# Mixing of a two-layer hybrid block: Gelus put off past the scans, steps reordered, the recurrence's elementwise steps moved from GpSimd

## The chip, the cores and the metric

One Trainium2 chip, one of its cores. The time is the device time of one execution of the program, in microseconds (us); lower is better. A core has TensorE (PE in the profile; PEld is its weight load), VectorE (DVE), ScalarE (ACT), GpSimd (POOL) and SyncE (SP, which here issues almost all transfers). Each runs its own queue of instructions in order and waits on semaphores for the others.

## What is computed

Two layers over 512 latent tokens and 256 context tokens of width 1024, all in fp32. Each layer has a token-mixing and a SwiGLU part; the change touches the mixing alone. One input projection feeds three head groups:

```python
# A: bidirectional gated recurrence on 512 channels, gated by gelu of 512 more
xc = conv4(p[..., :512])
r, i = sigmoid(xc @ wa + ba), sigmoid(xc @ wx + bx)          # per direction
a = exp(-8 * r * softplus(-lam))
h = scan(a, sqrt(1 - a*a) * (i * xc))                        # both directions, added
y_a = gelu(p[..., 512:1024]) * h
# B: chunked gating on 256 channels
u, v = gelu(p[..., 1024:1280]), gelu(p[..., 1280:1536])
y_b = u * (ws @ layer_norm(v) + bs)
# C: Fourier mixing on 256 channels
y_c = real(fft2(p[..., 1536:])) @ wf
out = concat(rms(y_a), rms(y_b), rms(y_c)) @ w_out
```

The last layer gives no context output, so its gate, u, v and Fourier parts cover the 512 latent tokens only; its recurrence covers all 768.

## The kernel before

Tokens lie in six tiles of 128. A product in fp32 is made of three products of rounded halves (`mm`, lines 195 to 200), so every operand is split into a high half (a rounding copy, mostly ScalarE's, line 208) and a low half (a subtraction, line 203). Weights are split as they come to be used; during the mixing `self.wsub` puts the low half of a weight on GpSimd, until the step `D` puts it on VectorE. PSUM holds three large tiles (`mm`, 1024 wide) and two small ones (`aux`, 512 wide).

The order of the mixing is written out by hand: `mixing` (line 959) walks the string `STEPS[l]` (line 49) and calls one step for each letter. Loads follow the same string (`plan`) and are issued by SP ahead of use, as far as the arena has room; a digit sets the room that loads must leave. The letters:

- `e`: the four gate products of one group of 128 recurrence channels, their sigmoids, and i times xc (line 751); `a`, `k`: projection, convolution and split of the fourth group; `f`: Fourier maps.
- `Z`, `V`, `U`: weights for z, v, u are taken and split. `z`: a Fourier projection, split out of PSUM (lines 819 and 820). `c`: Fourier products over channels for two tiles, split out of PSUM the same way. `v`, `u`: a projection for two tiles and its Gelu (line 921); v is then normalised on VectorE (`gating_norm`).
- `p`: Tanh and Exp of one recurrence group, both directions (`lru_scans`, lines 764 and 767). It leaves two pieces of work; `s` runs one of them: Sqrt (773), four elementwise operations (774 to 777), two scans (781 to 785); the second adds both directions (791).
- `g`: the projection of a gate, its Gelu (1000), times h (1002), squared (1003), the squares summed (1005).
- `m`: 512 columns of the modulation, 2 MB of weights, copied out of PSUM (515); the part before is then transposed and reduced (`mod_put`). `R`: two such parts become rows, added to broadcast rows of b_mod (547, loaded at line 551).
- `w`, `t`: the gating's matrices and its products (953); then come the products over positions of the Fourier part (`fourier`) and the output projection.

ScalarE holds one set of function tables at a time; Sigmoid, Tanh with Exp, Sqrt, and Gelu each need a load (ACT_TABLE_LOAD in the profile). `in_turn` and `behind` keep ScalarE's functions in the order of the steps, so that these loads stay few.

## Time and profile before

| | |
|---|---|
| median of 3 runs | 1561.46 us (1560.18 to 1562.3) |
| the profiled execution | 1561.9 us, its span 1559.8 us |
| TensorE, matmul | 1447.0 us busy (93%) |
| VectorE | 781.7 us (50%) |
| ScalarE | 531.5 us (34%) |
| GpSimd | 349.2 us (22%) |
| mean granted clock of TensorE | 0.967 |
| DMA | 163.59 MB, 105 GB/s on the mean |

The span runs from the first instruction to the last. Busy times are sums over one execution. The rows that count are further down, ahead of the prediction.

### The profile page before, as it was taken

To read this page: it belongs to the slowest core of one execution; us is meant where nothing else is said; L and a number is where in the kernel's file an instruction comes from. 1 tells how busy PE (TensorE), PEld (TensorE's weight loads), DVE (VectorE), ACT (ScalarE), POOL (GpSimd) and SP (SyncE) were. 2 spreads that over 40 slices of the span, in tenths; PEclk is the share of its full clock that TensorE was granted. 3 is DMA by queue.
4 is the path that set the end of the run, shared out by engine and by line. 5 is a ranking of instruction groups with operands and counts; after the bars stand their busy time and mean duration, and the time that the engine had idled before them with its cause. 6 is when DMAs were issued, how large, how long until landed. Compare 5 with 4: busy or idle time off the path is not lost. (4 is left out here: it accounts for less than half of the span.)

```text
span 1559.8 us, 19102 instructions
## 1 busy us (share of the span) xinstructions
PE 1447.0 (93%) x7735; PEld 1199.8 (77%) x7735; DVE 781.7 (50%) x1183; ACT 531.5 (34%) x776; POOL 349.2 (22%) x226
## 2 busy tenths in 40 slices
PE   6993998999999999999999988948898999999997
PEld 3682977788888888888888878737777788888885
DVE  6739737874323322332324386297775442543327
ACT  4574325345202202212203146854526321322210
POOL 3335512230021030020030045543321021120101
PEclk9996999999999999999999999969899999999999
DMA  9404264216106225153127004014327341432201
GB/s 321 130 1 139 85 213 173 74 65 221 55 14 212 72 96 174 55 182 111 32 79 220 14 1 135 7 41 135 103 68 238 107 135 55 128 100 78 73 0 54
DMA packets 169432, 163.59 MB, mean 105 GB/s; under 512 B 10456, under 2 KB 126648, under 8 KB 169344
## 3 DMA queue, kind: packets, MB, share of 16 engines
q1 hardware_dynamic: 169232, 162.08, 33.0%
q8 instruction: 61, 1.00, 0.3%
q0 software_dynamic: 112, 0.30, 0.1%
q14 instruction: 27, 0.22, 0.1%
HBM read 160.25 MB, written 2.10 MB: 104 GB/s over the span
## 5 line engine op out<-in xcount | busy, mean ns | idle before, releaser
L134 PE MATMUL mm<-r,r 128*128 128x512 f32 (+1 forms) x6192 | 1234.9, 360 | 18.9 <-DVE f L1138 9.2
L134 PEld LDWEIGHTS mm<-r,r 128*128 128x128 f32 x6192 | 1035.4, 191 | 214.3 <-DVE f L1138 15.0
L208 ACT ACTIVATE r<-f 128x1024 fp32r<-128x1024 f32 (+3 forms) x257 | 226.8, 908 | 626.6 <-PE mm L134 287.5
L203 DVE TENSOR_TENSOR r<-f,r 128x1024 fp32r<-128x1024 f32 (+3 forms) x262 | 275.3, 1077 | 221.0 <-ACT r L208 200.8
L203 POOL TENSOR_TENSOR f<-f,f 128x1024 f32<-128x1024 f32 (+2 forms) x68 | 153.2, 2254 | 758.1 <-DVE f L1138 565.6
L1153 DVE TENSOR_TENSOR f<-mm,f 128x768 f32<-128x768 f32 (+1 forms) x44 | 36.3, 825 | 252.8 <-PE mm L134 219.7
L1138 DVE TENSOR_TENSOR f<-mm,f 128x512 f32<-128x512 f32 (+1 forms) x80 | 76.3, 953 | 146.0 <-PE mm L134 145.9
L134 PE MATMUL aux<-r,r 128*128 128x256 f32 (+1 forms) x780 | 111.6, 304 | 39.9 <-DVE r L820 33.8
L134 PEld LDWEIGHTS aux<-r,r 128*128 128x128 f32 x780 | 105.0, 208 | 49.5 <-DVE r L820 35.7
L232 POOL TENSOR_TENSOR smalls<-smalls,neghalf 128x1 f32<-128x1 f32 (+2 forms) x69 | 65.1, 946 | 258.1 <-DVE smalls L231 255.6
L203 POOL TENSOR_TENSOR r<-f,r 128x512 fp32r<-128x512 f32 (+2 forms) x55 | 97.9, 1785 | 93.9 <-ACT r L414 28.1
L1152 ACT ACTIVATE f<-mm 128x768 f32<-128x768 f32 (+1 forms) x44 | 30.8, 700 | 121.8 <-PE mm L134 121.7
L134 PE MATMUL aux<-f,stc 128*32 128x512 f32 x384 | 51.9, 630 | 14.5 <-DVE r L820 11.3
L601 ACT ACTIVATE f<-aux,modT 128x128 f32<-128x128 f32 x128 | 48.5, 466 | 39.3 <-PE aux L134 34.8
L134 PE MATMUL aux<-cst,f 128*128 128x128 f32 (+1 forms) x243 | 37.2, 284 | 24.5 <-ACT f L586 7.8
L134 PEld LDWEIGHTS aux<-cst,f 128*128 128x128 f32 (+1 forms) x243 | 28.3, 143 | 35.3 <-ACT f L586 10.1
L586 ACT ACTIVATE f<-f,smalls 128x1024 f32<-128x1024 f32 x19 | 23.6, 1241 | 88.3 <-DVE smalls L585 88.3
L774 DVE SCALAR_TENSOR_TENSOR f<-f,f 128x768 f32<-128x768 f32 x16 | 24.7, 1543 | 45.2 <-ACT f L773 45.2
L134 PEld LDWEIGHTS aux<-f,stc 128*32 128x32 f32 x384 | 10.4, 112 | 36.8 <-issue 18.7
L719 DVE SCALAR_TENSOR_TENSOR f<-mm,par,f 128x255 f32<-128x255 f32 (+3 forms) x48 | 26.0, 607 | 15.2 <-ACT f L713 15.2
L775 POOL TENSOR_SCALAR f<-f 128x768 f32<-128x768 f32 x16 | 22.8, 1426 | 42.8 <-DVE f L774 37.7
L203 DVE TENSOR_TENSOR f<-f,f 128x512 f32<-128x512 f32 (+1 forms) x42 | 31.3, 745 | 1.5 <-ACT f L1003 0.9
(105 smaller groups left out, 641.3 us busy)
## 6 DMA issues: line engine op xcount, KB each, us to landing
f<-in_w_mod_dram SPq DMA_DIRECT2D x96, 512.0 KB
f<-in_w_up_dram SPq DMA_DIRECT2D x88, 512.0 KB
f<-in_w_down_dram SPq DMA_DIRECT2D x40, 512.0 KB
f<-in_w_in_dram SPq DMA_DIRECT2D x28, 512.0 KB
f<-in_w_out_dram SPq DMA_DIRECT2D x16, 512.0 KB
f<-in_b_mod_dram SPq DMA_DIRECT2D x6, 512.0 KB
f<-in_x_dram SPq DMA_DIRECT2D x4, 512.0 KB
f<-in_k_sinl_dram SPq DMA_DIRECT2D x4, 512.0 KB
```

The lines of the kernel that those rows point to most:

```text
L134: i = f(*args, **kw)
L203: return eng.tensor_tensor(out=out, in0=a, in1=b, op=op)
L208: i = self.nc.scalar.activation(h, src, AF.Copy)
L232: self.nc.gpsimd.tensor_tensor(out=out, in0=v, in1=self.neghalf[:, 0:n], op=ALU.pow)
L586: nc.scalar.activation(n.f, x, AF.Identity, bias=nm, scale=r)
L601: nc.scalar.activation(y.f[:, q * P : (q + 1) * P], ps[:, q * P : (q + 1) * P], AF.Identity, bias=self.modT[:, slot, k, s : s + 1], scale= ...
L719: nc.vector.scalar_tensor_tensor(out=o, in0=ps[:, i0 : i0 + o1 - o0], scalar=w(k), in1=o, op0=ALU.mult, op1=ALU.add)
L774: nc.vector.scalar_tensor_tensor(out=t_.f, in0=r.f, scalar=1.0, in1=t_.f, op0=ALU.add, op1=ALU.mult)
L775: nc.gpsimd.tensor_scalar(out=t_.f, in0=t_.f, scalar1=-1.0, scalar2=1.0, op0=ALU.mult, op1=ALU.add)
L1138: self.nc.vector.tensor_tensor(out=tb.f, in0=ps[:, c], in1=m[:, c], op=ALU.mult)
L1152: nc.scalar.activation(g.f, pg[:, 256 + lo : 1024], AF.Silu)
L1153: nc.vector.tensor_tensor(out=g.f, in0=pu[:, 256 + lo : 1024], in1=g.f, op=ALU.mult)
```

## The change

Three things. Gelus: until the new step `L` the results of gate, v and u are copied out of PSUM as they are (the new `gelu`, with `self.hold` set), and the Gelu, and what follows it, is kept in `self.late`; `L` clears the flag and does the work kept. Steps: both strings are reordered. In layer 0 two gates, the v and the u stand among the scans, the c behind `L`. In layer 1 `L` stands ahead of the first v, so nothing is kept there; its first two `s` come ahead of the second `p`. Engines: lines 751 and 791 go from GpSimd to VectorE, line 775 (1 - x) to ScalarE as an Identity with scale -1 and bias 1.

```diff
--- before.py
+++ after.py
@@ -46,7 +46,7 @@
 BETWEEN = 2
 START_RESERVE = 11000
 MIX_RESERVE = (12000, 9000)
-STEPS = ("feaekZeeppsz6szsspmpcsssmc7cgVsvvUvuuuw7DgRmgmtgmm", "faeekeeZppsszszsppVccssvsvUugDsugwgtg")
+STEPS = ("feaekZeeppzssz6ssgpgpsssVvvsvUuuumgmcLccw7DRmtgmmm", "faeekeeZpsspszzsppLcVcssvsvgUuDsugwgtg")
 PARAMS_AT = 5
 NEXT_AT = {6: 0, 7: 2, 9: 1, 10: 3, 12: 6, 13: 7, 15: 8, 16: 9, 18: 4, 19: 5}
 
@@ -748,7 +748,7 @@
         xl.free()
         for d in range(2):
             i = gates[2 * d + 1]
-            self.tt(nc.gpsimd, i.f, i.f, xc.f, ALU.mult)
+            self.tt(nc.vector, i.f, i.f, xc.f, ALU.mult)
         xc.free()
         return gates, insts
 
@@ -772,7 +772,7 @@
             s = self.buf(TOK)
             self.in_turn([nc.scalar.activation(s.f, t_.f, AF.Sqrt)])
             nc.vector.scalar_tensor_tensor(out=t_.f, in0=r.f, scalar=1.0, in1=t_.f, op0=ALU.add, op1=ALU.mult)
-            nc.gpsimd.tensor_scalar(out=t_.f, in0=t_.f, scalar1=-1.0, scalar2=1.0, op0=ALU.mult, op1=ALU.add)
+            nc.scalar.activation(t_.f, t_.f, AF.Identity, bias=self.ones[:, 0:1], scale=-1.0)
             nc.vector.scalar_tensor_tensor(out=s.f, in0=r.f, scalar=1.0, in1=s.f, op0=ALU.add, op1=ALU.mult)
             nc.vector.tensor_tensor(out=s.f, in0=s.f, in1=i.f, op=ALU.mult)
             a, u, h = t_.f, s.f, i.f
@@ -788,7 +788,7 @@
             if d == 1:
                 lo = 256 if l == DEPTH - 1 else 0
                 out = hs[m] = self.buf(TOK)
-                self.tt(nc.gpsimd, out.f[:, lo:], gates[1].f[:, lo:], h[:, lo:], ALU.add)
+                self.tt(nc.vector, out.f[:, lo:], gates[1].f[:, lo:], h[:, lo:], ALU.add)
                 gates[1].free(LRU_LAG)
                 gates[3].free(LRU_LAG)
 
@@ -910,7 +910,22 @@
             self.drop(u)
         return put
 
-    def gating_in(self, tiles, half, pair, w):
+    def gelu(self, out, ps, then=None):
+
+        nc = self.nc
+
+        def rest(src):
+            self.behind([nc.scalar.activation(out, src, AF.Gelu)], self.turn)
+            if then is not None:
+                then()
+
+        if self.hold:
+            nc.scalar.activation(out, ps, AF.Copy)
+            self.late.append(lambda: rest(out))
+        else:
+            rest(ps)
+
+    def gating_in(self, tiles, half, pair, w, then=None):
 
         z = self.buf(512)
         ps = self.psum_aux()
@@ -918,7 +933,7 @@
             for k in range(KC):
                 o = ps[:, n * 256 : (n + 1) * 256]
                 self.mm(o, self.lhs_tok(tiles[2 * pair + n], k), tuple(x[:, k % 4, :] for x in w[k // 4]), k == 0, k == KC - 1)
-        self.behind([self.nc.scalar.activation(z.f, ps, AF.Gelu)], self.turn)
+        self.gelu(z.f, ps, (lambda: then(z)) if then is not None else None)
         return z
 
     def gating_norm(self, pair, z, vb):
@@ -980,7 +995,7 @@
                 parts[blk] = self.mod_part(l, blk)
 
         self.gw, gt, work, bd = [], [], [], []
-        self.turn = []
+        self.turn, self.late, self.hold = [], [], True
         done = {"e": 0, "p": 0}
 
         zt, zc, uv, ws = [], [], {"v": [], "u": []}, []
@@ -997,13 +1012,16 @@
             self.drop(u)
             g = self.buf(TOK)
             sq.append(g)
-            self.behind([nc.scalar.activation(g.f[:, lo:], ps[:, 256 + lo : 1024], AF.Gelu)], self.turn)
-            y = hs[m]
-            nc.vector.tensor_tensor(out=y.f[:, lo:], in0=y.f[:, lo:], in1=g.f[:, lo:], op=ALU.mult)
-            nc.scalar.activation(g.f[:, lo:], y.f[:, lo:], AF.Square)
-            if m > 0:
-                self.tt(nc.gpsimd if m < MA - 1 else nc.vector, sq[0].f[:, lo:], sq[0].f[:, lo:], g.f[:, lo:], ALU.add)
-                g.free()
+
+            def rest():
+                y = hs[m]
+                nc.vector.tensor_tensor(out=y.f[:, lo:], in0=y.f[:, lo:], in1=g.f[:, lo:], op=ALU.mult)
+                nc.scalar.activation(g.f[:, lo:], y.f[:, lo:], AF.Square)
+                if m > 0:
+                    self.tt(nc.gpsimd if m < MA - 1 else nc.vector, sq[0].f[:, lo:], sq[0].f[:, lo:], g.f[:, lo:], ALU.add)
+                    g.free()
+
+            self.gelu(g.f[:, lo:], ps[:, 256 + lo : 1024], rest)
 
         def step(x):
             if x in "ZVU":
@@ -1053,6 +1071,10 @@
                     self.mod_rows(parts.pop(4 + hf), hf, m2, not last)
             elif x == "t":
                 self.gating(tiles, uv["u"], vb, ws)
+            elif x == "L":
+                self.hold = False
+                while self.late:
+                    self.late.pop(0)()
             elif x == "D":
                 self.wsub = nc.vector
             elif x == "g":
@@ -1064,9 +1086,7 @@
                     vb.extend([self.buf(n_t * 256), self.buf(n_t * 256)])
                 w = [tuple(b.r.rearrange("p (k n) -> p k n", n=256) for b in (u.high, u.low)) for u in held[x]]
                 pair = len(uv[x])
-                uv[x].append(self.gating_in(tiles, x, pair, w))
-                if x == "v":
-                    self.gating_norm(pair, uv["v"][pair], vb)
+                uv[x].append(self.gating_in(tiles, x, pair, w, (lambda z: self.gating_norm(pair, z, vb)) if x == "v" else None))
                 if pair == n_t // 2 - 1:
                     for u in held[x]:
                         self.drop(u)
```

How the instructions stand now, in three places. In these rows a name such as `f_768_746` is an arena buffer (columns, then a number given at its creation); `r_` names hold halves for products; `aux` and `mm` are PSUM. Line numbers of the changed kernel are some 1 to 20 higher behind the new function: 923 is the plain copy, 918 the Gelu, 1018 the old 1002.

ScalarE, layer 0, from the first group's Sqrts on, before:

```order
L773 ACTIVATE f_768_632<-f_768_880 128x768
L773 ACTIVATE f_768_1012<-f_768_884 128x768
L773 ACTIVATE f_768_1020<-f_768_886 128x768
L764 ACT_TABLE_LOAD
L764 ACTIVATE f_768_1030<-f_768_811,spl 128x768
L767 ACTIVATE f_768_811<-f_768_811,spl 128x768
L819 ACTIVATE r_768_640<-mm 128x768
L764 ACTIVATE f_768_1032<-f_768_829,spl 128x768
L767 ACTIVATE f_768_829<-f_768_829,spl 128x768
L764 ACTIVATE f_768_1063<-f_768_866,spl 128x768
L515 ACTIVATE f_512_1059<-aux 128x512
L764 ACTIVATE f_768_1061<-f_768_848,spl 128x768
```

And with the change:

```order
L773 ACTIVATE f_768_1020<-f_768_886 128x768
L775 ACTIVATE f_768_880<-f_768_880,ones 128x768
L208 ACTIVATE r_1024_1030<-f_1024_459 128x1024
L819 ACTIVATE r_768_640<-mm 128x768
L208 ACTIVATE r_1024_1034<-f_1024_190 128x1024
L764 ACT_TABLE_LOAD
L764 ACTIVATE f_768_746<-f_768_829,spl 128x768
L775 ACTIVATE f_768_884<-f_768_884,ones 128x768
L208 ACTIVATE r_1024_451<-f_1024_462 128x1024
L767 ACTIVATE f_768_829<-f_768_829,spl 128x768
L775 ACTIVATE f_768_886<-f_768_886,ones 128x768
L923 ACTIVATE f_768_1098<-mm 128x768
```

Weight splits (208) for the gates and for v have moved up among the Sqrts, Tanhs and Exps, each Sqrt is followed after a few rows by an Identity (775) that needs VectorE's line 774, and the plain copy of gate 0 (923) stands behind them.

VectorE, layer 0, in the second group's scans, before:

```order
L782 SCALAR_TENSOR_TENSOR f_768_770<-f_768_884,f_768_770,f_768_1012 128x512
L784 SCALAR_TENSOR_TENSOR f_768_788<-f_768_886,f_768_1020 128x256
L820 TENSOR_TENSOR r_512_1075<-aux,r_512_1074 128x512
L785 SCALAR_TENSOR_TENSOR f_768_788<-f_768_886,f_768_788,f_768_1020 128x512
L820 TENSOR_TENSOR r_512_1086<-aux,r_512_1085 128x512
L774 SCALAR_TENSOR_TENSOR f_768_1030<-f_768_811,f_768_1030 128x768
L776 SCALAR_TENSOR_TENSOR f_768_880<-f_768_811,f_768_880 128x768
L774 SCALAR_TENSOR_TENSOR f_768_1032<-f_768_829,f_768_1032 128x768
L777 TENSOR_TENSOR f_768_880<-f_768_880,f_768_820 128x768
L776 SCALAR_TENSOR_TENSOR f_768_632<-f_768_829,f_768_632 128x768
```

And with the change, the same group and the begin of the next:

```order
L781 SCALAR_TENSOR_TENSOR f_768_770<-f_768_884,f_768_1012 128x256
L777 TENSOR_TENSOR f_768_1020<-f_768_1020,f_768_788 128x768
L782 SCALAR_TENSOR_TENSOR f_768_770<-f_768_884,f_768_770,f_768_1012 128x512
L784 SCALAR_TENSOR_TENSOR f_768_788<-f_768_886,f_768_1020 128x256
L785 SCALAR_TENSOR_TENSOR f_768_788<-f_768_886,f_768_788,f_768_1020 128x512
L203 TENSOR_TENSOR f_768_1028<-f_768_770,f_768_788 128x768
L774 SCALAR_TENSOR_TENSOR f_768_1100<-f_768_811,f_768_1100 128x768
L776 SCALAR_TENSOR_TENSOR f_768_1163<-f_768_811,f_768_1163 128x768
L774 SCALAR_TENSOR_TENSOR f_768_746<-f_768_829,f_768_746 128x768
L777 TENSOR_TENSOR f_768_1163<-f_768_1163,f_768_820 128x768
```

The two splits of Fourier columns (820, out of `aux`) are gone from among the scans; the addition of both directions (203, called at 791) has come in.

ScalarE, layer 1, from the first group's Tanh on, before:

```order
L764 ACTIVATE f_768_7243<-f_768_7371,spl 128x768
L767 ACT_TABLE_LOAD
L767 ACTIVATE f_768_7353<-f_768_7353,spl 128x768
L767 ACTIVATE f_768_7371<-f_768_7371,spl 128x768
L764 ACTIVATE f_768_7513<-f_768_7391,spl 128x768
L764 ACTIVATE f_768_7515<-f_768_1061,spl 128x768
L767 ACTIVATE f_768_7391<-f_768_7391,spl 128x768
L767 ACTIVATE f_768_1061<-f_768_1061,spl 128x768
L773 ACT_TABLE_LOAD
L773 ACTIVATE f_768_7255<-f_768_7508 128x768
L773 ACTIVATE f_768_666<-f_768_7243 128x768
L819 ACTIVATE r_768_7560<-mm 128x512
```

And with the change:

```order
L767 ACT_TABLE_LOAD
L767 ACTIVATE f_768_7414<-f_768_7414,spl 128x768
L764 ACTIVATE f_768_7375<-f_768_7396,spl 128x768
L767 ACTIVATE f_768_7396<-f_768_7396,spl 128x768
L773 ACT_TABLE_LOAD
L773 ACTIVATE f_768_7557<-f_768_7375 128x768
L773 ACTIVATE f_768_7565<-f_768_7553 128x768
L764 ACT_TABLE_LOAD
L764 ACTIVATE f_768_7575<-f_768_7434,spl 128x768
L775 ACTIVATE f_768_7375<-f_768_7375,ones 128x768
L775 ACTIVATE f_768_7553<-f_768_7553,ones 128x768
L764 ACTIVATE f_768_7577<-f_768_7452,spl 128x768
```

The first two Sqrts come ahead of the second group's Tanh and Exp, with a table load more on the way back, and two Identities stand between.

## Rows read from the trace of the kernel before

**Rows 1.** The page, busy time: us, share of the span, instructions.

```profile
PE 1447.0 (93%) x7735; PEld 1199.8 (77%) x7735; DVE 781.7 (50%) x1183; ACT 531.5 (34%) x776; POOL 349.2 (22%) x226
```

**Rows 2.** Stretches: us, busy PE, PEld, DVE, ACT, POOL (instructions), clock, DMA, GB/s.

```profile
200.00:250.50 50.50, 44.68 (x273) 32.28 (x271) 25.25 (x53) 20.50 (x35) 6.92 (x8) 0.98 0.66 229
116.70:250.50 133.80, 103.20 (x676) 82.92 (x676) 95.01 (x186) 51.99 (x85) 48.99 (x28) 0.89 0.46 156
1013.05:1107.58 94.53, 61.18 (x344) 53.10 (x345) 79.23 (x137) 50.26 (x74) 40.74 (x25) 0.81 0.25 84
```

**Rows 3.** Waits of PE, 116.7 to 250.6, then 1013 to 1107.7: sum, times, longest.

```profile
PE aux L134 <- DVE r L820: 21.5, 2, 11.3
PE aux L134 <- ACT f L515: 2.6, 3, 1.4
PE aux L134 <- DMA f<-in_w_mod_dram: 2.0, 1, 2.0
PE aux L134 <- DVE r L816: 1.8, 1, 1.8
...
PE aux L134 <- DVE r L820: 23.7, 5, 10.9
```

**Rows 4.** Timeline, PE, layer 0: start, us, engine, line, operation, count, [idle before].

```profile
94.84 21.86 PE L134 MATMUL mm<-r,r 128*128 128x256 f32 x124
...
151.44 3.42 PE L134 MATMUL aux<-r,r 128*128 128x256 f32 x12 [10.15 <-DVE r L820]
```

**Rows 5.** Timeline, VectorE, layer 0's scans.

```profile
112.48 0.96 DVE L774 SCALAR_TENSOR_TENSOR f<-f,f 128x768 f32<-128x768 f32 x1 [17.56 <-ACT f L773]
...
125.85 2.55 DVE L774 SCALAR_TENSOR_TENSOR f<-f,f 128x768 f32<-128x768 f32 x1
...
129.19 1.57 DVE L776 SCALAR_TENSOR_TENSOR f<-f,f 128x768 f32<-128x768 f32 x1
...
171.05 0.93 DVE L1002 TENSOR_TENSOR f<-f,f 128x768 f32<-128x768 f32 x1
```

**Rows 6.** Groups by line, GpSimd, 95 to 172: count, busy us, mean ns, idle before.

```profile
L203 POOL TENSOR_TENSOR r<-f,r 128x1024 fp32r<-128x1024 f32 x5 | 15.2, 3052 | 3.8 <-ACT r L208 3.8
L775 POOL TENSOR_SCALAR f<-f 128x768 f32<-128x768 f32 x8 | 11.9, 1490 | 20.8 <-DVE f L774 20.8
```

**Rows 7.** Timeline, PE, layer 0: c, u, a gate, m.

```profile
140.30 0.98 PE L134 MATMUL aux<-r,r 128*128 128x256 f32 x6 [0.51 <-ACT f L515]
...
194.00 6.02 PE L134 MATMUL aux<-r,r 128*128 128x256 f32 x48 [0.34 <-ACT f L921]
...
200.22 8.60 PE L134 MATMUL mm<-r,r 128*128 128x256 f32 x48
...
237.50 1.92 PE L134 MATMUL aux<-f,stc 128*32 128x512 f32 x16
```

**Rows 8.** Timeline, ScalarE, layer 0: the first Sqrt and its table load.

```profile
110.24 1.28 ACT L773 ACT_TABLE_LOAD   x1
111.54 0.85 ACT L773 ACTIVATE f<-f 128x768 f32<-128x768 f32 x1
```

**Rows 9.** Timeline, SP and PE, layer 0: loads of b_mod's rows and step R.

```profile
198.65 1.74 SPq L551 DMA_DIRECT2D f<-in_b_mod_dram  x2
...
208.65 1.08 PE L134 MATMUL aux<-r,sel 128*128 128x512 f32 x4
```

**Rows 10.** Timeline, VectorE and PE, layer 1: the first scan step, c, a gate.

```profile
1013.33 0.96 DVE L774 SCALAR_TENSOR_TENSOR f<-f,f 128x768 f32<-128x768 f32 x1 [24.08 <-ACT f L773]
...
1022.88 1.01 PE L134 MATMUL aux<-r,r 128*128 128x256 f32 x3 [7.81 <-DVE r L820]
...
1027.47 1.86 PE L134 MATMUL aux<-r,r 128*128 128x256 f32 x7 [3.58 <-DVE r L820]
...
1040.27 2.93 PE L134 MATMUL aux<-r,r 128*128 128x256 f32 x12 [10.93 <-DVE r L820]
...
1061.08 5.63 PE L134 MATMUL mm<-r,r 128*128 128x512 f32 x24
```

## The prediction

> **What bounds the kernel now.** I read four views: the page's head, the table of stretches, the waits, the timeline. The head [rows 1] says that TensorE (PE) is the bound, busy 1447.0 of 1559.8 us; what an order can win is the rest, and what a low clock adds. The table of stretches [rows 2] finds much of it in the mixing of both layers. Layer 0, from the end of the second Fourier projection (step z) to the first product over positions: 133.8 us, PE busy 103.2 of it, at a clock of 0.89. Layer 1, likewise: 94.5 us, busy 61.2, at 0.81.
>
> The list of waits [rows 3] names what PE waits for: nearly always line 820, VectorE's low half of a split out of PSUM, 21.5 us in two waits in layer 0 and 23.7 us in five in layer 1. The timeline places them. PE's last z product ends at 94.84 + 21.86 = 116.7; after a few products it idles 11.3 us [rows 3], and before 151.44 another 10.15 [rows 4]. Its next work, the Fourier columns (step c), frees its two PSUM buffers only through line 820. That instruction stands in VectorE's queue among the scans, which run from 112.48 to 171.05 [rows 5]: 58.6 us for four channel groups, 14.6 each.
>
> Part of this is GpSimd's doing. A VectorE operation on 128x768 takes 0.95 us by itself and 2.55 beside GpSimd's addition (line 791), 1.57 beside its line 775 [rows 5]: 1.6 and 0.62 us lost each time. Per layer GpSimd does eight of 775 there, and four of 791 [rows 6]; the halves of weights that it also makes, 3.05 us each, stay with it.
>
> **The change, part by part.**
>
> *The change of the orders, layer 0.* All PE work stays; its places change. At the times at full clock [rows 7] it is 6 m of 1.92, 6 c of 0.98, 4 gates of 8.6, 6 u and v of 6.02, and about 12 us of small transposes and sums: 99.9. So the stretch now loses 133.8 - 99.9 = 33.9 us. After the change two gates and all v and u, 53 us of work that needs no VectorE result, follow the z, and the c come when the scans are through. What then is lost:
> - Gate 0's weights are split by ScalarE behind four Sqrts and two of the new Identities: from 111.54 [rows 8] six times 0.85 makes 116.6, their Copy 1 us, GpSimd 3.05: 120.7. PE waits 4.0.
> - The second v unit is split into space that the scan of group 1 gives back, and ScalarE waits for it. VectorE needs 14.6 - 2 x 0.62 - 1.6 + 0.95 = 12.7 us a group now (its own addition counted); that scan ends at 112.5 + 12.7 + 8 = 133, the halves come at 137.5 to 140, PE at 120.7 + 2 x 8.6 + 1.5 = 139.4. 1.5 us.
> - v's third copy stands behind group 3's Sqrt and Identity, a table load and a Gelu: 112.5 + 3 x 12.7 + 8 + 4.4 = 163. PE, at its fourth aux tile, is there at 163.4. 1.5 us.
> - The put-off work (six Gelus of u and v, two of gates, three norms on VectorE of some 6 us) begins at about 165 and ends at 187; m's copy is behind it. PE gets to c at 189. 1 us, and 2.5 in c itself, whose six evacuations follow one another closely.
> - Step R needs two b_mod rows. Now they are issued when PE is through with u; after the change they wait for c's last products. They were issued at 198.65 and used at 208.65, a gate of 8.6 us between [rows 9]; then R follows c and w at once. 4 us.
> - Gate 1 no longer parts the last three m: one more wait of 1.4 us for a copy. The waits that stay, 2.6 us for line 515 and 1.8 for line 816 the largest [rows 3], make 6.
>
> Sum 21.9, gain 12 us. The added copies cost ScalarE 9 passes of 0.6 to 0.85, 6 us, hidden, since it is busy 52 of these 133.8 us [rows 2].
>
> *The change of the orders, layer 1.* Work there: 4 c, 4 u and v, 4 gates of 5.63 [rows 10], 5.6 of small things: 56.1, so 38.4 us are lost. Nothing is put off (L comes before the first gate, v or u); the first scan pieces come ahead of the second group's Tanh and Exp. Two Tanh and two Exp, four passes of some 0.85, no longer stand ahead of the first Sqrt, so VectorE starts at 1009.9, not 1013.33 [rows 10]. The two z splits move behind one more piece; they end at about 1023.5, against the waits that end at 1022.88 and 1027.47 now. The evacuations of the first two c follow at 1033, not 1040.27 [rows 10]: the scans of group 1 are through earlier, and GpSimd blocks less. PE is then 6.5 us ahead. Of the 12 us lost behind that point I take 1.5 as saved. Gain 8 us.
>
> A price in this is table loads. Sqrt and Tanh or Gelu alternate more often: eleven loads instead of nine. One takes 1.28 us, and the next operation starts 0.02 after it [rows 8]: 2.6 us more of ScalarE, inside the times above. The Trainium skill, ScalarE: Activation LUTs, section What ACT_TABLE_LOAD costs, gives 2.66 us for a switch, as a drain of 1.38 goes with the load; that makes 5.3 us, and with all of it on PE's path the sum would be 2.7 us smaller. The row shows no drain, so I keep 1.28.
>
> *GpSimd's steps.* The product of line 751 goes to VectorE before the scans, where that is idle (17.6 us before its first scan step, [rows 5]): nothing, and if that cover went, 8 x 0.95 = 7.6 us a layer. Line 775 costs ScalarE 8 x 0.85 = 6.8 us a layer, in order behind VectorE's 774. No row shows this Identity. The Sqrt of the same size, engine and kind of memory is nearest, 0.85 [rows 8], and I take it; GpSimd's own 1.49 [rows 6] is the upper end, and 0.64 x 8 = 5 us more a layer. Line 791 is counted above.
>
> Sum: 20 us off. The profiled execution took 1561.9 us (span 1559.8), 0.4 above the median of the runs, so 1561.9 - 20 = about **1542**.
>
> The bounds: with every estimated wait in layer 0 at zero but the old 6, it gains 28; with each doubled, -4. Layer 1 lies between 0 (c no earlier) and 16.
>
> **Rivals.**
>
> *The wait moves to ScalarE.* Its queue is in order. Identity and Sqrt wait for VectorE there, and the copies that free PE's PSUM tiles are queued behind. If the scans end no earlier than now (171), the second v, the fourth aux tile and c each come 6 to 8 us later: layer 0 gains nothing, and layer 1, where table loads lie between, 5: 1557. For it: the order of ScalarE's queue, and that two terms above are met by 0 to 3 us only. Against it: GpSimd's share of the scans' delay goes. 0.22.
>
> *PE is covered throughout.* VectorE loses much less than 12.7 a group without GpSimd, ScalarE is never late: layer 0 gains 24, layer 1 14: 1524. Against it are the weights of the first gate, whose 4 us follow from rows. 0.09.
>
> *Slower: the modulation weights come late.* Two gates leave the part after the scans, and four m with 2 MB each stay. At 229 GB/s [rows 2] a block takes 9.2 us, its products 1.92. Three m now end the steps in a row, and their last block's buffers come free only with gating (step t). If the queue of SP is no further ahead than its buffers allow, each of four m waits up to 7.3, less the 5 of R and gate 3: +24, so 1542 + 24 = 1566. It decides from the point where loads are issued less than 9 us before use on all four. For it: the DMA engines are busy 0.66 of the time from 200 to 250 [rows 2]. Against it: one wait of 2.0 us for these weights now [rows 3], and the third and fourth m's blocks can be issued when v and u leave. 0.07.
>
> **Numbers.** The forecast has 0.62. Its own range is 1532 to 1554, by the terms above (8 to 30 us). With the rivals, 1529 to 1559 leaves out about 0.2: the slower case, most of the covered one, and a little at the edge of ScalarE's. A run tells 0.2% (3.1 us) from no change. Faster: 0.62, 0.09 and 0.16 of the first rival, 0.87; the same: 0.06, the rest of it; slower 0.07.
>
> **What the profile will show if this is right.** In layer 0 no wait of PE for line 820 over 2 us between 117 and 185; gate matmuls from about 118 to 138; clock near 1.00 there; VectorE's last scan at 160 to 166 and not 171; the first product over positions at about 238; PE waits for ScalarE's copies in place of 820, and some us for VectorE at 547 behind b_mod. In layer 1 the first 774 some 3 us earlier after the gates, c done about 7 us sooner, the products over positions 8 us closer to the gates. No row of GpSimd at 775. Wrong, if PE's waits for ScalarE in the scans of layer 0 pass 12 us, or if waits for w_mod appear.

## Result and the profile after

The changed kernel takes 1537.61 us (median of 4 runs, 1536.49 to 1539.31) where the kernel before takes 1560.82 beside it: a ratio of 0.9854, with a 95% interval of 0.9837 to 0.9872. That is 23.2 us less. The forecast was 1542, 19.5 us below the median that it started from, with a range of 1529 to 1559. The profiled execution took 1537.34 us, its span 1535.3, so 24.5 us less than the span of before.

Where the 24.5 us came from, by the table of stretches (us, busy time of PE, PEld, DVE, ACT and POOL with instructions, granted clock, DMA share, GB/s), of the kernel after. The first two rows answer to the last two of [rows 2]; the third is the first half of layer 0's stretch.

```profile
117.18:240.16 122.98, 104.10 (x677) 83.00 (x677) 92.88 (x188) 63.80 (x101) 34.22 (x18) 0.94 0.52 169
1001.70:1084.83 83.13, 59.09 (x345) 52.21 (x345) 71.46 (x137) 59.44 (x84) 19.80 (x12) 0.85 0.34 111
117.20:185.00 67.80, 59.01 (x415) 54.71 (x416) 59.42 (x97) 37.46 (x50) 27.50 (x10) 0.95 0.34 104
```

Layer 0, from the end of z to the first product over positions, went from 133.8 to 123.0 us: 10.8 less. Layer 1 went from 94.5 to 83.1: 11.4 less. What is left of the 24.5 is small: 0.5 more ahead of layer 0's stretch, 1.0 less between the two, 1.8 less behind the second. The granted clock rose from 0.89 to 0.94 in layer 0 and from 0.81 to 0.85 in layer 1; in the third row it is 0.95, where the forecast had near 1.00. The page's busy times, to be held against [rows 1]: GpSimd (POOL) loses 61 us, ScalarE gains 22.

```profile
PE 1443.5 (94%) x7735; PEld 1195.7 (78%) x7735; DVE 785.1 (51%) x1206; ACT 553.6 (36%) x803; POOL 288.0 (19%) x187
```

The waits of PE (sum, times, longest), in layer 0's stretch of the kernel after:

```profile
PE aux L134 <- ACT f L923: 4.7, 1, 4.7
PE aux L134 <- ACT f L515: 3.3, 4, 1.2
PE mm L134 <- POOL r L203: 2.0, 1, 2.0
PE aux L134 <- DVE f L547: 1.9, 2, 1.7
PE aux L134 <- DVE r L816: 1.9, 2, 1.6
...
PE aux L134 <- DVE r L820: 1.0, 3, 0.4
```

and in layer 1's:

```profile
PE aux L134 <- DVE r L820: 8.8, 3, 6.8
PE aux L134 <- ACT r L819: 6.9, 1, 6.9
PE aux L134 <- DVE f L203: 3.2, 1, 3.2
```

Against [rows 3], line 820 fell from 21.5 to 1.0 us in layer 0 and from 23.7 to 8.8 in layer 1. In its place stand ScalarE's copies: line 923, the new plain copy of v, and line 819, the high half of z's split.

PE's timeline after, in layer 0 and, in the last row, at layer 1's second pair of c (start, us, engine, line, operation, count, [idle before]):

```profile
120.64 18.10 PE L134 MATMUL mm<-r,r 128*128 128x256 f32 x94 [2.05 <-POOL r L203]
140.59 17.53 PE L134 MATMUL aux<-r,r 128*128 128x256 f32 x144 [0.30 <-POOL r L203]
...
168.13 13.27 PE L134 MATMUL aux<-r,r 128*128 128x256 f32 x96 [4.73 <-ACT f L923]
...
206.28 1.30 PE L134 MATMUL aux<-r,sel 128*128 128x512 f32 x2 [1.71 <-DVE f L547]
207.78 1.22 PE L134 MATMUL aux<-r,sel 128*128 128x512 f32 x2 [0.20 <-DVE f L547]
...
1021.10 15.18 PE L134 MATMUL aux<-r,r 128*128 128x256 f32 x108 [6.77 <-DVE r L820]
```

Two gates and then v and u fill the time in which PE idled before [rows 4]. VectorE's timeline in layer 0, however, is not what was forecast (the last row is the first step of layer 1's scans):

```profile
112.50 0.96 DVE L774 SCALAR_TENSOR_TENSOR f<-f,f 128x768 f32<-128x768 f32 x1 [1.20 <-ACT f L773]
...
118.31 3.37 DVE L782 TENSOR_TENSOR_SCAN f<-f,f,f 128x512 f32<-128x512 f32 x1
121.60 2.80 DVE L784 TENSOR_TENSOR_SCAN f<-f,f 128x256 f32<-128x256 f32 x1
...
138.38 2.98 DVE L203 TENSOR_TENSOR f<-f,f 128x768 f32<-128x768 f32 x1
144.65 0.96 DVE L774 SCALAR_TENSOR_TENSOR f<-f,f 128x768 f32<-128x768 f32 x1 [3.29 <-ACT f L773]
...
168.97 1.28 DVE L785 TENSOR_TENSOR_SCAN f<-f,f,f 128x512 f32<-128x512 f32 x1
...
998.84 0.96 DVE L774 SCALAR_TENSOR_TENSOR f<-f,f 128x768 f32<-128x768 f32 x1 [6.01 <-ACT f L773]
```

The scans run from 112.50 to 170.25, 57.8 us, where they took 58.6 before [rows 5]. They are hardly shorter. GpSimd's groups from 95 to 172 (count, busy, mean ns, idle before) give one reason, against [rows 6]:

```profile
L203 POOL TENSOR_TENSOR r<-f,r 128x1024 fp32r<-128x1024 f32 x7 | 22.4, 3210 | 79.8 <-ACT r L208 67.4 <-issue 12.4
```

Lines 775 and 791 are gone, but the new order brings more low halves of weights: seven in this window in place of five. The seventh begins at 171.47, when the scans are through, so six stand among the scans.

The other reason is the row at 144.65: VectorE waits 3.29 us for the Sqrt of the third group. ScalarE's timeline shows where that Sqrt stands:

```profile
136.52 1.06 ACT L208 ACTIVATE r<-f 128x1024 fp32r<-128x1024 f32 x1 [4.09 <-DVE f L782]
...
143.71 1.58 ACT L773 ACTIVATE f<-f 128x768 f32<-128x768 f32 x2
```

The high half of a weight (line 208) waits on ScalarE for space that the second group's scan gives back. Three Exps, two Tanhs, the copy of gate 1 and a table load stand behind it, and then the Sqrt.

Layer 0's gain with scans as long as before looks like the order's alone. The runs show that it isn't.

### The profile page after: what moved, and what is told of

The parts are those of the page before. It is cut to its first block, busy times and chain, and to the rows that moved or that the text cites. A ratio compares the mean times of both kernels' runs of the same rounds, so it can differ in the third digit from the quotient of the medians.

```text
span 1535.3 us, 19073 instructions
## 1 busy us (share of the span) xinstructions
PE 1443.5 (94%) x7735; PEld 1195.7 (78%) x7735; DVE 785.1 (51%) x1206; ACT 553.6 (36%) x803; POOL 288.0 (19%) x187
## 5 line engine op out<-in xcount | busy, mean ns | idle before, releaser
L203 DVE TENSOR_TENSOR r<-f,r 128x1024 fp32r<-128x1024 f32 (+3 forms) x261 | 270.7, 1065 | 191.0 <-ACT r L208 159.5
L203 POOL TENSOR_TENSOR f<-f,f 128x1024 f32<-128x1024 f32 (+2 forms) x44 | 106.3, 2416 | 681.2 <-DVE f L1158 638.0
L203 POOL TENSOR_TENSOR r<-f,r 128x512 fp32r<-128x512 f32 (+2 forms) x56 | 101.5, 1820 | 209.4 <-ACT r L208 142.8
L203 DVE TENSOR_TENSOR f<-f,f 128x512 f32<-128x512 f32 (+1 forms) x66 | 60.6, 920 | 11.1 <-ACT f L743 8.3
L134 PE MATMUL aux<-cst,f 128*128 128x128 f32 (+1 forms) x243 | 37.1, 283 | 24.5 <-DVE f L339 7.3
L565 DVE BATCH_NORM_STATS2 smalls<-f 128x6 f32<-128x512 f32 x44 | 28.4, 682 | 5.9 <-DMA f<-in_ctx_dram 5.6
L743 ACT ACTIVATE f<-mm,par 128x768 f32<-128x768 f32 x32 | 28.0, 902 | 5.0 <-PE mm L134 3.7
```

Of the source, the lines that this page charges most:

```text
L134: i = f(*args, **kw)
L203: return eng.tensor_tensor(out=out, in0=a, in1=b, op=op)
L565: nc.vector.bn_stats(out=st[:, c, :], in_=x[:, c * 512 : (c + 1) * 512])
L743: insts.append(nc.scalar.activation(g.f, ps[:, 256:1024], AF.Sigmoid, bias=par[:, col : col + 1]))
```

## Experiments

All times are medians; the kernel before ran beside each and took 1561.3 to 1562.4. Each ratio is to that kernel. Where a run is set against the change, the intervals of two ratios together leave some 3 us, so a difference of 1 or 2 us is not resolved. "The scans" are the time from the first 774 to the end of the last 785 in layer 0; stretches are those of one profiled execution.

**The moves alone.** The kernel before, with

```diff
-self.tt(nc.gpsimd, i.f, i.f, xc.f, ALU.mult)
+self.tt(nc.vector, i.f, i.f, xc.f, ALU.mult)
-nc.gpsimd.tensor_scalar(out=t_.f, in0=t_.f, scalar1=-1.0, scalar2=1.0, op0=ALU.mult, op1=ALU.add)
+nc.scalar.activation(t_.f, t_.f, AF.Identity, bias=self.ones[:, 0:1], scale=-1.0)
-self.tt(nc.gpsimd, out.f[:, lo:], gates[1].f[:, lo:], h[:, lo:], ALU.add)
+self.tt(nc.vector, out.f[:, lo:], gates[1].f[:, lo:], h[:, lo:], ALU.add)
```

> The kernel before with only the three edits that take steps from GpSimd (lines 751, 775, 791); both strings of steps as before. Theory 1, that of the prediction (GpSimd holds VectorE up: 1.9 us a group in layer 0, so the split that PE waits for comes 5 us sooner there, and 3 in layer 1): 1553 us, some 8 less than before, and PE's waits for line 820 fall from 21.5 to about 16 in layer 0 and from 23.7 to 20 in layer 1. Rival A (the low halves of weights that stay on GpSimd hold VectorE up just as much, and the Identity on ScalarE costs what the rest gives): within 2 us of before, the last scan of layer 0 at 170 to 172 as before. Rival B (ScalarE's queue becomes the wait): 1565, waits for ScalarE in place of line 820.

Measured: 1550.06, ratio 0.9928 (0.9915 to 0.994), 11.2 us less. Theory 1, and more of it: PE's waits for line 820 fall to 10.7 us in layer 0, not 16, and to 21.8 in layer 1, not 20. Its stretches of the two layers and VectorE's scans:

```profile
116.39:245.55 129.16, 102.42 (x678) 81.91 (x677) 90.82 (x188) 57.71 (x92) 29.45 (x17) 0.92 0.48 161
1007.69:1095.73 88.04, 59.00 (x344) 52.05 (x345) 76.73 (x141) 57.18 (x82) 22.41 (x13) 0.83 0.27 90
```

```profile
111.08 0.96 DVE L774 SCALAR_TENSOR_TENSOR f<-f,f 128x768 f32<-128x768 f32 x1 [9.30 <-ACT f L773]
...
163.39 1.28 DVE L785 TENSOR_TENSOR_SCAN f<-f,f,f 128x512 f32<-128x512 f32 x1
```

In the old order the scans take 53.6 us, 5.0 less than before; layer 0's stretch is 4.6 shorter, layer 1's 6.5.

**The orders alone.** The changed kernel with the same three edits the other way round.

> The changed kernel with the three steps back on GpSimd: only the orders and the putting off stay. Theory 1 (the steps on GpSimd hold up VectorE, and GpSimd's own queue then also delays the weights of the first gate): 1548 us, 10 more than the change, of which some 4 in layer 0. Rival A (what GpSimd does in the scans is hidden once PE has other work): 1538 to 1541, layer 0 as long as in the change (123 us from the last z product to the first product over positions). If the two parts simply add, its gain over before and that of the moves alone sum to 23.

Measured: 1564.16, ratio 1.0016 (1.0007 to 1.0025), 2.9 us more than before. Neither theory: the orders by themselves win nothing, they lose. Layer 0's stretch and scans:

```profile
117.80:257.60 139.80, 109.12 (x677) 86.89 (x676) 93.44 (x186) 59.14 (x95) 50.54 (x29) 0.89 0.46 150
```

```profile
114.30 0.96 DVE L774 SCALAR_TENSOR_TENSOR f<-f,f 128x768 f32<-128x768 f32 x1 [1.26 <-ACT f L773]
...
151.42 0.96 DVE L774 SCALAR_TENSOR_TENSOR f<-f,f 128x768 f32<-128x768 f32 x1 [7.90 <-ACT f L773]
...
179.50 1.27 DVE L785 TENSOR_TENSOR_SCAN f<-f,f,f 128x512 f32<-128x512 f32 x1
```

The scans take 66.5 us. PE's new work waits for them after all, since the weights of v and u are split into space that a scan gives back, and the scans wait for ScalarE in their turn: the third group's Sqrt stands behind such a split, and VectorE waits 7.90 us for it (151.42). ScalarE's timeline in this run shows the high halves (line 208) waiting for the scan of line 782:

```profile
141.70 1.06 ACT L208 ACTIVATE r<-f 128x1024 fp32r<-128x1024 f32 x1 [7.70 <-DVE f L782]
...
159.84 1.06 ACT L208 ACTIVATE r<-f 128x1024 fp32r<-128x1024 f32 x1 [6.35 <-DVE f L782]
```

The two parts give -11.2 and +2.9 by themselves and -23.2 together. They are not two gains that add: the moves are worth 26.6 in the new orders.

What makes the scans long can be added up from VectorE's rows. By itself an operation on 768 columns takes 0.95 us, a scan of 512 columns 1.27, one of 256 columns 0.67; what a row is longer than that stands beside a GpSimd instruction in each case. In us:

| | scans | VectorE waits | rows longer beside GpSimd | its own work |
|---|---|---|---|---|
| before | 58.6 | 0.4 | 17.2 | 41.0 |
| the moves alone | 53.6 | 0.5 | 9.6 | 43.5 |
| the orders alone | 66.5 | 10.6 | 17.1 | 38.8 |
| the change | 57.8 | 4.3 | 12.6 | 40.9 |

So the orders alone do not slow VectorE beside GpSimd more than before: they make it wait, 9.9 of the 10.6 us for Sqrts. In the change both are smaller. Of its 12.6 us the six halves make all; the five halves of before made 9.1 of 17.2, three additions (791) 4.6 and six of the eight 775 3.5.

**One layer's new order.** First the changed kernel with layer 1's old string, then with layer 0's old string, nothing put off in the layer that is put back:

```diff
-STEPS = (NEW0, NEW1)
+STEPS = (NEW0, "L" + OLD1)
```

> The changed kernel with the old string in layer 1 (nothing is put off there). The trace of the change shows layer 0 some 11 us shorter and layer 1 some 11 shorter than before. Theory 1 (layer 1's gain is its new order, which starts the scans before the second pair of Tanh and Exp, with 1 or 2 us from GpSimd): 1537.6 + 9 = 1547 us. Rival A (layer 1's gain is mostly the steps that left GpSimd): 1541 or less.

```diff
-STEPS = (NEW0, NEW1)
+STEPS = ("L" + OLD0, NEW1)
```

> The changed kernel with the old string in layer 0 (Gelus at once there). Theory 1 (layer 0's gain is gates, v and u that PE does during the scans; the moves alone give some 3 to 5): 1537.6 + 7 = 1545 us. Rival A (the moves give nothing in layer 0, since its last scan ends at 170.2 instead of 171.0): 1548 to 1549. Rival B (the moves alone give most of it): 1540 or less.

Measured: 1551.61 (0.9941, 0.9927 to 0.9954) and 1549.82 (0.993, 0.9917 to 0.9942), 14.0 and 12.2 above the change; each theory 1 asked for some 5 less. The second agrees with the moves alone: layer 1's new order shortens its stretch by 3 more (85.0 for 88.0) and that hardly shows in the time. It comes near its rival A, whose reason does not hold: in the moves alone layer 0's stretch is 4.6 shorter. In the first, layer 1 is 7.8 us longer than in the moves alone, with the same string and the same engines. Its stretch, and two waits that the moves alone do not have there:

```profile
1004.26:1100.09 95.83, 62.68 (x345) 55.35 (x345) 73.19 (x140) 54.72 (x79) 21.77 (x12) 0.76 0.24 77
```

```profile
PE mm L134 <- ACT r L208: 3.8, 1, 3.8
PE mm L134 <- POOL r L203: 2.2, 1, 2.2
```

The splits of weights stand at other places of ScalarE's queue there, two of them 3 and 5 us earlier after the end of z, a gate's later, and the clock is 0.76 for 0.83. That layer 0 leaves other room in the arena would explain it; it wasn't tried by itself, and what part each has stays open. Neither layer's new order adds a gain to the moves by itself (1551.61 and 1549.82 for 1550.06), and both together add 12.4: layer 1's new string shortens its stretch by 3 us behind layer 0's old string, and by 12.7 behind the new one (95.8 to 83.1).

**Each step back on GpSimd.** The changed kernel with one of the three lines as before: 775, then 791, then 751.

> The changed kernel with line 775 (1 minus a squared term) back on GpSimd, lines 751 and 791 stay on VectorE. With all three back the time was 1564.2, 26.6 above the change. Theory 1 (what counts is GpSimd's queue in order: 775 stands there behind the low halves of weights, 3 us each, and beside it each VectorE operation takes 0.62 longer, in layer 0 and layer 1): 1548 us, some 10 above the change; VectorE waits for 775 before scans. Rival A (the additions of line 791, 1.6 us lost by VectorE each time, are the larger part): 1542 or less. Rival B (ScalarE is relieved of 13 us and it is as fast): 1536 to 1539.

> The changed kernel with line 791 alone back on GpSimd. Theory 1 (a VectorE operation takes 1.6 us longer beside it, but VectorE is spared 0.95, and four of them a layer are all; GpSimd's queue is otherwise empty): 1541 us, 3 to 4 above the change. Rival A (this is the larger part of the 26.6 that all three make): 1550 or more. Rival B (nothing, as the addition leaves VectorE's queue): 1537 to 1539.

> The changed kernel with line 751 (i times xc) alone back on GpSimd. Line 775 back cost 7.3 us, line 791 4.8, all three 26.6. Theory 1 (751 runs before the scans, when GpSimd and VectorE have nothing else; the missing 14.5 us come from 775 and 791 standing together in one queue, each late behind the other and behind the weights): within 2 us of the change, 1536 to 1540. Rival (751 holds up the weights' low halves and the first scans' data, and so the start of the scans, by 2 us or more in each layer): 1543 or more.

Measured: 1544.89 (0.9902, 0.9886 to 0.9917), 1542.38 (0.9879, 0.9866 to 0.9893) and 1543.76 (0.9885, 0.9871 to 0.9898): 7.3, 4.8 and 6.1 above the change, 18.2 of the 26.6 that all three make. So none is free; which is the largest is not resolved. With 775 back the scans take 63.3 us, 5.5 more, and eight rows beside it that are longer by 0.5 to 0.6 make 4.8 of that, as theory 1 said; in layer 0 VectorE does not wait for 775 itself, and the time lies between theory 1 and rival A. With 791 back the time is what theory 1 said, but not by its means: the rows beside GpSimd are longer by 12.9 us in place of 12.6, and VectorE waits 9.9 us for Sqrts in place of 4.3, most of it at the third group, whose Sqrts begin at 146.98 in place of 143.71:

```profile
147.92 0.96 DVE L774 SCALAR_TENSOR_TENSOR f<-f,f 128x768 f32<-128x768 f32 x1 [7.97 <-ACT f L773]
```

For 751 the rival holds. With it back, the first step of the scans starts later, at 114.62 (112.50 in the change, 111.78 to 113.77 in the other runs of this order with 751 on VectorE), and in layer 1 the last z product ends 2.8 us later after layer 0's stretch (764.3 us for 761.5):

```profile
114.62 0.96 DVE L774 SCALAR_TENSOR_TENSOR f<-f,f 128x768 f32<-128x768 f32 x1 [1.26 <-ACT f L773]
```

The last 785 of these three begins at 175.02, 172.82 and 171.09, and the products over positions at 245.93, 245.28 and 242.43. In the change it is 168.97 and 240.16; in the orders alone 179.50 and 257.60.

**Gelus at once.** The changed kernel with the step L at the start, and a room of 7 for 6.

```diff
-"feaekZeeppzssz6ssgpgpsssVvvsvUuuumgmcLccw7DRmtgmmm"
+"LfeaekZeeppzssz7ssgpgpsssVvvsvUuuumgmcccw7DRmtgmmm"
```

> The changed kernel with Gelus at once in layer 0 too: the step L stands at the start of the string, the rest of the order stays; the room that loads leave there is 7 instead of 6, since buffers live otherwise. Theory 1 (ScalarE loads six more function tables of 1.28 us in layer 0, each ahead of a Sqrt, Tanh or Exp that the scans wait for, and the norms of v, 2 us each on VectorE, go among the scans; the new order is bound by the scans' speed): 1547 us, some 9 above the change. Rival (ScalarE was idle for 30 of the 68 us in which the scans run, so the loads fit in): within 2 us of the change.

Measured: 1563.92, ratio 1.002 (1.0011 to 1.0029), 26.3 us above the change: all of the gain goes, three times what theory 1 asked. ScalarE's timeline from one gate's Gelu to its Square (1019), and VectorE's where the third group's scans begin:

```profile
131.04 1.28 ACT L918 ACT_TABLE_LOAD   x1
132.34 0.81 ACT L918 ACTIVATE f<-mm 128x768 f32<-128x768 f32 x1
133.17 1.28 ACT L767 ACT_TABLE_LOAD   x1
...
139.52 0.84 ACT L1019 ACTIVATE f<-f 128x768 f32<-128x768 f32 x1 [4.12 <-DVE f L1018]
```

```profile
154.22 0.96 DVE L774 SCALAR_TENSOR_TENSOR f<-f,f 128x768 f32<-128x768 f32 x1 [7.29 <-ACT f L773]
...
185.31 1.28 DVE L785 TENSOR_TENSOR_SCAN f<-f,f,f 128x512 f32<-128x512 f32 x1
```

The loads alone would be 7.7 us. The scans take 74.8 us, 17.1 more than in the change. What the trace shows beside the loads is order: the Square waits 4.1 us on ScalarE for VectorE's product with h (1018), and splits, Tanhs, Exps and the Sqrt stand behind it. VectorE in turn waits 5.8 us for the next gate's Gelu and 7.3 for the Sqrt, and norms of v stand among the scans. The third group starts 9.6 us later than in the change (154.22 for 144.65). The loads and the order were not tried apart.

**Three attempts at a better order.** Each is a string only: in layer 1 everything put off; in layer 0 the third v earlier and R one m later; in layer 1 the z split earlier.

```diff
-"faeekeeZpsspszzsppLcVcssvsvgUuDsugwgtg"
+"faeekeeZpsspzzsscpVcpssvvsUuusgLDgwgtg"
```

> A new string for layer 1 that does there what the change does in layer 0: the z products before the second pair of Tanh and Exp, c before the third, v and u as copies, all Gelus after the last scan but one gate's (ZpsspzzsscpVcpssvvsUuusgLDgwgtg). ScalarE then loads 7 tables in place of 11. PE's waits after the last z product in layer 1 of the change are 6.9 for the split by ScalarE behind Tanh and Exp, 1.6 and 0.5, and 6.8 for VectorE's low half. Theory 1 (these waits are places in the queues and not work that is missing): 1531 us, 6 to 7 less than the change. Rival A (the scans set the end of layer 1, as the gates wait for them): 1536 to 1539. Rival B (the put-off pile of Gelus and norms comes before the product over positions and costs what is won): 1540 or more.

```diff
-"feaekZeeppzssz6ssgpgpsssVvvsvUuuumgmcLccw7DRmtgmmm"
+"feaekZeeppzssz6ssgpgpsssVvvvsUuuumgmcLccw7DmRtgmmm"
```

> A new string for layer 0 in two places: all three v before the last scan piece but one (Vvvvs for Vvvsv), and step R behind one more m (mR for Rm). In the change PE waits 4.7 us for v's third copy, which stands behind a Sqrt that waits for VectorE, and some 3.4 us between c and R, of which 1.7 for b_mod's row. Theory 1 (both are places in a queue): 4 to 6 us less than the change, 1532 to 1534; no wait over 1 us for a copy of v, none for line 547. Rival A (the copy ahead delays the last Sqrt and with it the put-off work, and c waits as long): 1537 to 1539. Rival B (R late holds the blocks of the modulation's loads): 1541 or more.

```diff
-"faeekeeZpsspszzsppLcVcssvsvgUuDsugwgtg"
+"faeekeeZpsszzpsscppLVcssvsvgUuDsugwgtg"
```

> A new string for layer 1: the split of z ahead of the second pair of Tanh and Exp, the first c ahead of the third (ZpsszzpsscppLVcssvsvgUuDsugwgtg for ZpsspszzsppLcVcssvsvgUuDsugwgtg). In the change PE waits 6.9 us for that split by ScalarE after the last z product. Theory 1 (the wait is a place in ScalarE's queue; z ends while it is idle or in Tanh): the first Fourier columns start some 4 us earlier, and the second pair no later: 1533 to 1535. Rival A (the scans set the end of layer 1, whatever PE does before): 1536 to 1540. Rival B (ScalarE stands waiting for the last z product, the scans of the second group start 2 us later, and all that follows them too): 1541 or more.

Measured: 1544.20 (0.9893, 0.988 to 0.9907), 1560.39 (0.9991, 0.9978 to 1.0003) and 1545.32 (0.9885, 0.9867 to 0.9902). All miss theory 1. In the first, line 819's wait is cut to 4.7, but line 820's stays at 6.2 and later waits are new (layer 1: 86.3 us, 3.1 more than in the change; the time behind it is 3.8 longer). In the last, PE no longer waits for ScalarE's split at all, and waits 6.6 for VectorE's half of it instead: that stood among the scans. Layer 1 is 85.3 us, 2.2 more; but of the 8.5 us that its profiled execution is longer, 5.1 lie up to the end of layer 0's stretch, where the string is the change's, so the 7.7 us of the medians are not shown to be this order's. The middle one failed by something else than it was to test. PE's row and ScalarE's, in layer 0:

```profile
191.12 0.79 PE L134 MATMUL mm<-r,r 128*128 128x256 f32 x2 [8.67 <-ACT r L208]
```

```profile
190.02 1.05 ACT L208 ACTIVATE r<-f 128x1024 fp32r<-128x1024 f32 x1
```

In the change, the third gate's weights are split at 170.34, ahead of the put-off norms; here they come behind them, at 190.02. The scans end as before (170.29), the gate is 8.7 us late, half of the 17.4 by which layer 0's stretch is longer (the rest is later waits and a clock of 0.85 for 0.94 behind the scans), and PE's wait for the copy of v is hardly shorter (3.9 for 4.7). Whether R one m later helps was not shown.

**Halves on VectorE.** The changed kernel with the step D right after layer 0's first gate, so that the low halves of four weights leave GpSimd.

```diff
-"feaekZeeppzssz6ssgpgpsssVvvsvUuuumgmcLccw7DRmtgmmm"
+"feaekZeeppzssz6ssgDpgpsssVvvsvUuuumgmcLccw7Rmtgmmm"
```

> The changed kernel with the step D right after the first gate of layer 0 instead of behind w: the low halves of four weights (both of v's second unit and u's, and the third gate's) are made by VectorE and not by GpSimd. In the change a VectorE operation beside such a half takes some 2.1 us longer (L203 128x768 2.98 in place of 0.95), and VectorE makes one by itself in 1.23. The runs so far show layer 0 of the new order ending some 70 us after the last scan whenever that comes (170.3: 240.2; 172.4: 242.4; 174.1: 245.3; 176.3: 245.9), so the scans still set it. Theory 1: three of the halves lie in the scans, each gives VectorE 2.1 back and takes 1.23: the last scan ends some 2.5 us earlier, at 167 to 168, and the time falls by about 2, to 1534 to 1537. Rival A (the halves stand in VectorE's queue behind scans, v and u wait for them): 1540 or more, PE's waits for line 203 of VectorE over 4 us. Rival B (GpSimd's halves cost VectorE nothing that counts): the scans end later, by 3 us, and so does the time: 1540.

Measured: 1535.97 (1534.24 to 1537.95), ratio 0.9833 (0.982 to 0.9847): 1.6 below the change, which the two intervals do not resolve. Theory 1 holds in its direction for the scans: they take 56.3 us (113.77 to 170.07), 1.5 less and not 2.5. VectorE's rows are longer beside GpSimd by 6.4 us in place of 12.6, it makes three halves at 1.2 itself, and it waits 5.1 us in place of 4.3. Layer 0's stretch is as long as in the change (122.8 for 123.0). PE's timeline shows why no more came of it:

```profile
175.73 1.93 PE L134 MATMUL aux<-f,stc 128*32 128x512 f32 x16
...
193.24 5.56 PE L134 MATMUL aux<-r,r 128*128 128x256 f32 x24 [4.29 <-ACT f L515]
```

The wait for the copy of v is gone, and PE reaches its first m 5.6 us earlier (175.73 for 181.33). It then waits 4.3 for the copy of an m, which stands on ScalarE behind the put-off Gelus and norms. These begin when the scans end.

## Why the prediction was right, and where it was not

The total was right in sign and nearly in size; its two layers were 12 and 8 us by forecast and 10.8 and 11.4 by measurement. That the total came so near is in part luck, since the step on the scans failed and other errors made up for it. Term by term:

- *The account of what bounded the kernel* held: line 820's split among the scans. It no longer makes PE wait over 0.4 us in layer 0.
- *The scans, 12.7 us a group and through at 163 (last scan at 160 to 166).* Wrong: 14.4 a group, through at 170.25, so 7 us late. Three things were mis-sized. The forecast took off eight of 775 and four of 791, 11.4 us; in the rows of before six and three of them slow VectorE, by 8.1. It left the halves as they were; the new order puts six among the scans in place of five, and the rows beside them are longer by 12.6 us in place of 9.1 (rows 118.31 and 121.60 above are 3.37 and 2.80 for scans of 1.27 and 0.66). And it priced ScalarE's wait for the scan's space for PE alone, at 1.5; the third group's Sqrt stands behind that split too, and VectorE's waits are 4.3 us in place of 0.4. The splits of line 820 that left the scans give part of it back. In the old order the moves bring the scans to 13.4 a group.
- *What the stretch loses, 21.9 us.* It lost 18.9 against PE's busy 104.1, which was forecast at 99.9, all at full clock; the clock was 0.94. The two errors nearly cancel, which is luck. Of the waits, gate 0's weights made 3.0 (forecast 4.0), the second v unit 0.3 (1.5), the aux tile behind v's third copy 4.7 (1.5; the copy is later with the scans), c 1.4 and nothing ahead of it (3.5), R 3.4 (4).
- *Layer 1, 6.5 at v's start and 1.5 later.* The first 774 came 2.9 us ahead of the last z product, not 0.3 behind it: 3.1 earlier, as forecast. The second pair of c went on 19.4 us after z, not 27.2: 7.8 sooner. Behind that 3.6 were saved for the 1.5 taken. How much of it is the order's is not one number: with the old string the moves alone give 6.5 of the 11.4, but behind layer 0's new string the old one gives none of it (95.8 us for 94.5 before).
- *GpSimd's steps cost nothing where they go.* The Identity took 0.93 on ScalarE, not the 0.85 of the Sqrt taken, 1.3 us over sixteen. For 751 "nothing" missed a gain: with that line back the time is 6.1 us longer.
- *Table loads.* Layer 1 has eleven, at 1.28 each. The Trainium skill, ScalarE: Activation LUTs, section What ACT_TABLE_LOAD costs, would have 2.66 for a switch; here too the next operation begins 0.02 after the load, and the load right after the operation before it (131.04, 132.34, 133.17 in the run with Gelus at once), so the trace bears out 1.28.

*The rivals.* "The wait moves to ScalarE" asked that the scans end no earlier and that layer 0 then gain nothing. Its first half came true (170.25), and so in part did its reason: VectorE waits for a Sqrt in ScalarE's queue. Its second half didn't come true. Call the rest the time from the end of the last scan to the first product over positions. It is 79.4 us before, 80.9 with the moves alone and 81.4 with layer 0's old string. In the new order it is 69.9 in the change, 69.4 to 72.0 in six other runs with the Gelus put off, and 71.4 with them at once. Three runs of that order lie outside: 73.9 with the z split earlier, at a clock of 0.89 there for 0.94; 76.8 in the orders alone, where PE waits 7.1 for the copy of a u; 87.3 with the third v earlier, where a gate's weights are late. So the order does two things. It takes some 10 us of PE's work from behind the scans to beside them, and it makes the scans longer, because of what that work needs of GpSimd and of ScalarE. Without the moves the second is larger: the scans take 66.5 us for 58.6 and the rest is only 2.6 shorter. With the moves the scans are about as long as before, and the first is the gain. The slower rival, modulation weights that come late, did not come: PE has no wait for w_mod in the stretch.

The forecast counted the moves inside the order's terms, as a small part of layer 0. By the runs the change has no part that could be left out: the orders without the moves lose 2.9 us, the rest without the putting off loses 2.4, and the moves without the orders keep 11.2 of 23.2.

## What to carry to other kernels

When an order brings work from behind a chain to beside it, count what that work asks of the chain's own engines, of the queues that feed the chain, and of the space that the chain gives back: the chain may grow by as much as was won. A split that waits for the chain's space holds up what stands behind it in its queue, and here that was the chain's own next step. Test the parts of such a change together and apart, since the sum of the parts can have the other sign. And in an order tuned by hand a letter moved is not one edit: look where the splits of weights land before the time is read as the verdict on the idea.

## What had not been expected

A low half of a weight on GpSimd delays VectorE by much the same time whatever VectorE does meanwhile, in the change by 2.0 to 2.2 us: a scan of 256 columns goes from 0.66 to 2.80, one of 512 from 1.27 to 3.37, an addition of 768 from 0.95 to 2.98. (In the moves alone two of five halves cost 1.5 and 1.6.) That is not a share of a common rate but a wait for the end of the other's instruction. The half beside the row at 138.38 ends at 140.55, and that row ends at 141.36, 0.8 later, where it takes 0.95 by itself. It goes both ways: a half at 129.33, beside VectorE's operations, takes 5.10 us itself, where the others take 2.8 to 3.0. The two halves beside the rows 118.31 and 121.60 are this row of GpSimd:

```profile
118.12 5.73 POOL L203 TENSOR_TENSOR r<-f,r 128x1024 fp32r<-128x1024 f32 x2 [46.00 <-ACT r L208]
```

Line 820, which reads one of its two inputs from PSUM, is not held up where the traces have it beside a half. In the kernel before it keeps its 0.68 us beside two halves, and the scan of 256 columns right behind it does not keep its 0.67:

```profile
158.73 5.85 POOL L203 TENSOR_TENSOR r<-f,r 128x1024 fp32r<-128x1024 f32 x2
...
159.49 0.68 DVE L820 TENSOR_TENSOR r<-aux,r 128x512 fp32r<-128x512 f32 x1
160.09 2.29 DVE L781 TENSOR_TENSOR_SCAN f<-f,f 128x256 f32<-128x256 f32 x1
```

The Trainium skill, SBUF — State Buffer, section Who interferes with whom, says that a VectorE instruction with two inputs in SBUF contends with a GpSimd instruction that reads SBUF, and that this contention is an exclusive lock. The trace agrees, with the 2.0 to 2.2 us above.

One execution's stretch is uncertain by some us: the run with the z split earlier has the instructions of the change in layer 0 and began its products over positions at 245.27, 5.1 later, at a lower clock (0.89 for 0.94 behind the scans). The length of the scans is steadier: 57.7 to 57.8 us in this run, in the change, and in the four others that alter only layer 1, line 751, or the third v and R.
